# One core, hybrid decoder layer with a PEER expert stage: the activation sums of the expert stage take four PSUM rooms in turn instead of two

## The chip, the core and the metric

The kernel runs on one core of a Trainium2 chip. The metric is the device time of one execution in microseconds (us). Five engines take part: PE (TensorE, the matmul engine), DVE (VectorE), ACT (ScalarE), POOL (GpSimd) and SP (SyncE, which here only issues loads). Matmul sums land in PSUM, which has eight rooms of 128 x 512 float32 values; the kernel names them b0 to b7 in its last part. DVE and ACT read the sums out of PSUM and thereby free the room.

## The reference

One layer on 256 tokens of width 2048. A first part (adaptive norm, one input projection, sparse attention and retention heads, output projection) makes `x`; it is not touched. The second part is a retrieval over 16,384 single-neuron experts:

```
def peer_ffn(h, w_q, sub_keys, w_u, w_v):
    q = (hf @ w_q).reshape(T, PEER_HEADS, 2, PEER_QUERY_DIM // 2)
    s_half = jnp.einsum('thpd,hpkd->thpk', q, sub_keys)
    v_half, i_half = lax.top_k(s_half, K)                # 16 best of 128 keys, twice
    ...
    top_s, pick = lax.top_k(cand_s, K)                   # 16 best of the 256 pairs
    gates = jax.nn.softmax(top_s, axis=-1)
    ...
        a = jnp.einsum('cd,ced->ce', hc, w_u[ec])
        coef = (gc * jax.nn.gelu(a))
        return jnp.einsum('ce,ced->cd', coef, w_v[ec])
```

Each token uses 8 x 16 = 128 experts. The result is gated, added to `x` and normalised.

## The kernel before

Most tokens are not gathered for but computed against all experts: the activations `u @ h` of every expert are formed, passed through gelu, multiplied by a gate matrix that is zero except at the chosen experts, and multiplied with `v`. Of the 256 tokens 160 (`TU`) go this way through `u` and 192 (`TD`) through `v`; the rest are served by gathered rows (`gather`, `steps_`, lines 799 to 869), which POOL fetches by index and DVE multiplies, one 128 x 2048 row block per step (line 844 for `u` rows, 850 for `v` rows).

The expert stage runs in this order: the query projection and the top-k search (lines 1080 to 1151, sums `psA` and `pss`), then for each half `hf` of the 128 expert blocks an activation stage (`u_half`, line 1238) and a value stage (`v_group`, line 897). In short U0, V0, U1, V1.

An activation stage goes through 64 blocks. `u_block` (line 1056) loads 1 MB of `u`, lets PE sum 16 matmuls of 128 x 160 into one room of PSUM (`psU`, line 1062), and has ACT apply gelu, either straight into the result `X` (line 1064, for the columns not yet gated) or into a small buffer `ge` with three places (line 1067), which DVE multiplies into `X` (line 1068). The room is free when ACT has read it.

Between the blocks come the gate groups, eight tokens each: DVE builds one-hot matrices (`o`, lines 1017 to 1020; for the last four groups of a stage `o1m`, `o2m`, `o2n`, lines 1034 to 1037), PE multiplies them into the gate matrix `pg` (line 1047), DVE multiplies it into those columns of `X` that have an activation (line 1052), and ACT copies it into the others (line 1054). In U0 the groups come after the remaining top-k work (`pick`, `gates`, `gates_exp` with an Exp on ACT, line 1179), which DVE does while the first blocks run.

A value stage goes through 64 blocks too: ACT and DVE split 1 MB of `v` into two float32r parts (`whi` line 946, `wlo` line 947), and PE adds 20 matmuls of 128 x 512 into eight sums at once (`acc`, line 964), one in each room: the second token tile's four quarters in b7 to b4, the first tile's in b3 to b0. At the end of V0 the eight sums are copied to SBUF in the order b7, b6 ... b0, ACT and DVE in turn (line 982).

The rooms of PSUM in this part are given out by `bank(kind)` (line 884), with a counter per kind: G (`pg`) takes b2 and b3 in turn, S (small things) b4 and b5, A (`psA`, and before the change `psU`) b6 and b7. Nothing but the value stages' sums uses b0 and b1.

What runs in which order on an engine is fixed before the run by the framework's scheduler, which works from its own estimate of when each room, buffer and operand is free. Some instructions are pinned to the program's order (loads of the stream, gathers, the gathered-row products). Each engine then works through its list strictly in that order.

Of the kernel before, what the change touches and what calls it, by code (L numbers as in the profile page):

```python
# [9 lines left out]
F32 = mybir.dt.float32  # L10
# [10 lines left out]
P = 128  # L21
# [27 lines left out]
TU = TD - NM  # L49
# [66 lines left out]
def body(ctx, tc, a, out, dbg=None, stop=None):  # L116
# [29 lines left out]
    def load(src):  # L146
        r = raw_tile()
        i = nc.sync.dma_start(r, src)
        if ring:
            tc.keep_in_program_order(i)  # L150
        return r
# [88 lines left out]
    def t_block(pool, src_chunk, tag="A", **kw):  # L240
        return t_blocks(pool, [src_chunk], (tag,), **kw)[0]
# [36 lines left out]
    with ExitStack() as fctx:  # L278
# [163 lines left out]
        def n_tile(i, src="winN", tag="A", pace="tile"):  # L442
            ps = [pp.tile([P, 512], F32, name="psN", tag=tag) for _ in range(2)]
            for c in range(4):
                hi, lo = split(load(a[src][i, c].rearrange("p k e -> p (k e)")))
                for kk in range(4):
                    k = 4 * c + kk
                    w = slice(kk * 512, (kk + 1) * 512)
                    for tt in range(2):
                        ts_ = slice(tt * P, (tt + 1) * P)  # L450
                        for j, (x, y) in enumerate(((hh, hi), (hh, lo), (hl, hi))):
                            nc.tensor.matmul(ps[tt], x[:, k, ts_], y[:, w], start=k == 0 and j == 0,  # L452
                                             stop=k == KB - 1 and j == 2)
                background(pace)
            return ps
# [62 lines left out]
        for gp in range(2):  # L518
# [3 lines left out]
            for r in range(4):  # L522
# [37 lines left out]
                f = lambda x: x.rearrange("p a b c d -> p (a b c) d")  # L560
# [142 lines left out]
        for q in range(4):  # L703
            sl = slice(q * 512, (q + 1) * 512)
            ps = n_tile(q, "woutN", "AS"[q % 2], "out")
# [23 lines left out]
        for k in range(KB):  # L729
            with tc.high_priority(offset=(KB - k) * 10):  # L730
                ps = pp.tile([P, 2, P], F32, name="psX", tag="TO"[k % 2])
# [3 lines left out]
                ps = ps.rearrange("p t s -> p (t s)")  # L735
# [8 lines left out]
    with ExitStack() as gctx:  # L744
# [21 lines left out]
        def xb(j):  # L766
            i = sum(j >= b for b in SEG) - 1
            return X[i][:, j - SEG[i], :]
# [115 lines left out]
        def bank(kind):  # L884
            turn[kind] += 1
            return f"b{dict(G=2, S=4, A=6)[kind] + turn[kind] % 2}"
# [169 lines left out]
        def u_block(pool, hf, j, done):  # L1056

            w = load(a["u"][hf * HALF + j].rearrange("p k e -> p (k e)"))
            ps = pool.tile([P, TU], F32, name="psU", tag=bank("A"))
            done = min(done, TU)  # L1060
            for k in range(KB):
                nc.tensor.matmul(ps, w[:, k * P:(k + 1) * P], xT[:, k, 0:TU], start=k == 0, stop=k == KB - 1)  # L1062
            if done < TU:
                nc.scalar.activation(xb(j)[:, done:TU], ps[:, done:TU], AF.Gelu_apprx_tanh)  # L1064
            if done > 0:
                ge = gp_.tile([P, TU], F32, name="ge", bufs=3)
                nc.scalar.activation(ge[:, 0:done], ps[:, 0:done], AF.Gelu_apprx_tanh)  # L1067
                nc.vector.tensor_mul(xb(j)[:, 0:done], xb(j)[:, 0:done], ge[:, 0:done])  # L1068
# [66 lines left out]
        for i in range(16):  # L1135
            ps = first[i] if i < 2 else t_block(up, wq(i), bank("A"), dst=early if i == 2 else None)
# [101 lines left out]
        def u_half(pool, hf, s2, work, budget):  # L1238
            groups[0] = 0
            credit = 0.0  # L1240
            for j in range(HALF):
                u_block(pool, hf, j, groups[0])
                credit += budget if hf or len(work) <= 16 + TD // 8 + 1 else 12.0
                while work and (credit >= work[0][0] or j == HALF - 1):
                    if not hf and j < 28 and len(work) <= TD // 8 + 1:
                        break
                    if not hf and len(work) <= NM // 8 + 1 and plan.index(("u", 1)) > len(plan) - left[0] - 1:
                        break
                    c, f = work.pop(0)
                    credit -= c  # L1250
                    f(j + 1)
                if j == 0:
                    if hf:
                        other[0], most[0] = third_room, 3
                        fetch()
                        set_ring(late, raw=5, whi=3)
                    else:
                        spare[0], other[0], most[0] = s2, more_room, 3
                        set_ring(late, raw=5, whi=3, wlo=2)
                if j == HALF - 10:  # L1260
                    other[0], most[0] = more_room, 3 - hf
                if j == HALF - 4:
                    set_ring(late, raw=5)
                if hf:
                    sparse(j in STEPS["u1"])
                else:
                    if j < 4:
                        rows_m(j)
                    sparse(j in STEPS["u0"])
# [4 lines left out]
        ps = up.tile([P, 512], F32, name="psh", tag=bank("S"))  # L1274
# [41 lines left out]
```

## Time and profile before

| | us |
|---|---|
| median of 3 runs (lowest, highest) | 1898.67 (1896.92, 1903.09) |
| the profiled execution, its own time | 1908.31 |
| the profiled execution, its span | 1906.5 |
| U0, first activation matmul to first value matmul | 688.1 to 996.5 |
| V0 | 996.5 to 1289.0 |
| U1 | 1289.0 to 1581.2 |
| V1, up to the last value matmul | 1581.2 to 1876 |
| PE busy, of the span | 1818.3 (95%) |

The profiled execution is one run; 1.8 us of its time lie around its span. All places below are in microseconds from the start of the span. A row of the timeline gives start, length, engine, line, operation, destination and sources, the number of instructions merged, and in brackets how long the engine idled before it and on what. One activation matmul of the code appears as two records in the trace, so a block of 16 is 32 records.

### The profile page before, as it was taken

Reading aid. Unit: us, or ns where it says so; the run is one execution under the profiler, and the core shown is the slowest. Engines: PE = TensorE matmul, PEld = TensorE weight load, DVE = VectorE, ACT = ScalarE, POOL = GpSimd, SP = SyncE. Lnnn points to the kernel's source line nnn. Section 1 sums busy time; section 2 is a strip of 40 time slices with the busy share of each in tenths; the row PEclk is TensorE's granted clock in tenths of the full one; section 3 lists DMA queues with packets and bytes.
Section 4 is the critical chain, followed back from the end, with each engine's and each line's share of the span. In section 5 each row is a group of like instructions: output and inputs, shape, how many; then the busy total and the mean of one; then the engine's idle time right before and its main releaser. Section 6 shows DMA issues by size and latency. Waiting matters only on the chain.

```text
span 1906.5 us, 28615 instructions
## 1 busy us (share of the span) xinstructions
PE 1818.3 (95%) x11303; PEld 1590.0 (83%) x11303; DVE 1480.8 (78%) x2333; ACT 708.4 (37%) x1279; POOL 370.8 (19%) x256
## 2 busy tenths in 40 slices
PE   5899999999998999999999999999999999999995
PEld 4899878788777898999997777779999997777773
DVE  7988877889788998677478899983455558988875
ACT  3444443635435421021025555541111114555542
POOL 1000001011000012102123343331111114544210
PEclk9999899999998999999999999999999999999998
DMA  8999877889797879988989999989999989999981
GB/s 350 373 328 370 303 278 225 314 286 350 288 352 259 318 292 355 410 352 338 382 318 380 416 411 418 415 322 425 375 357 365 347 328 382 418 384 391 382 300 45
DMA packets 94474, 652.93 MB, mean 342 GB/s; under 512 B 11410, under 2 KB 11618, under 8 KB 18434
## 3 DMA queue, kind: packets, MB, share of 16 engines
q1 hardware_dynamic: 66818, 467.78, 64.1%
q0 software_dynamic: 27520, 183.32, 24.5%
q8 instruction: 89, 1.46, 0.3%
q14 instruction: 47, 0.38, 0.1%
HBM read 644.97 MB, written 4.22 MB: 341 GB/s over the span
## 4 chain that ended last, share of the span: by engine, by line
PE 78%; DVE 13%; DMA 5%; issue 2%; ACT 1%; POOL 0%; SPq 0%; ACTq 0%; POOLq 0%; DVEq 0%
PE acc L964 31%; PE psU L1062 25%; PE psN L452 8%; DMA raw<-in_adaT 3%; DVE wlo L158 2%; PE bkB L353 2%; DVE raw L198 2%; PE psD L353 2%; PE bkC L353 1%; PE bvB L405 1%; PE psA L236 1%; PE pg L1047 1%; DMA raw<-in_winA 1%; PE pT L548 1%; PE sc L538 1%
## 5 line engine op out<-in xcount | busy, mean ns | idle before, releaser
L1062 PE MATMUL psU<-xT,raw 128*128 128x160 f32 x4096 | 573.1, 301 | 6.7 <-ACT X L1064 4.2
L1062 PEld LDWEIGHTS psU<-xT,raw 128*128 128x128 f32 x4096 | 561.6, 191 | 7.9 <-ACT X L1064 4.7
L964 PE MATMUL acc<-whi,cc 128*128 128x512 f32 x1512 | 367.9, 391 | 0.0
L947 DVE TENSOR_TENSOR wlo<-raw,whi 128x2048 fp32r<-128x2048 f32 x126 | 288.0, 2286 | 71.2 <-issue 57.8
L964 PEld LDWEIGHTS acc<-whi,cc 128*128 128x128 f32 x1512 | 283.8, 188 | 68.9
L964 PE MATMUL acc<-wlo,cc 128*128 128x512 f32 x1008 | 252.8, 391 | 2.4 <-DVE wlo L947 2.4
L946 ACT CAST whi<-raw 128x2048 fp32r<-128x2048 f32 x126 | 240.7, 1911 | 0.0
L157 ACT CAST whi<-raw 128x1024 fp32r<-128x1024 f32 (+1 forms) x174 | 168.5, 1017 | 187.2 <-PE psN L452 42.9
L198 DVE SCALAR_TENSOR_TENSOR raw<-raw,crow 128x2048 f32<-128x2048 f32 x96 | 219.1, 2284 | 23.6 <-DMA raw<-in_adaT 23.5
L158 DVE TENSOR_TENSOR wlo<-raw,whi 128x1024 fp32r<-128x1024 f32 (+1 forms) x174 | 200.8, 1180 | 27.4 <-ACT whi L157 27.3
L964 PEld LDWEIGHTS acc<-wlo,cc 128*128 128x128 f32 x1008 | 161.8, 161 | 63.6 <-DVE wlo L947 3.2
L452 PE MATMUL psN<-whi,act 128*128 128x512 f32 x512 | 172.3, 413 | 1.3 <-ACT whi L157 1.1
L1068 DVE TENSOR_TENSOR X<-X,ge 128x160 f32<-128x160 f32 (+19 forms) x94 | 25.8, 275 | 163.3 <-ACT ge L1067 161.3
L1064 ACT ACTIVATE X<-psU 128x160 f32<-128x160 f32 (+19 forms) x102 | 25.5, 252 | 320.7 <-PE psU L1062 308.7
L452 PEld LDWEIGHTS psN<-whi,act 128*128 128x128 f32 x512 | 97.9, 194 | 27.1 <-issue 3.2
L452 PE MATMUL psN<-wlo,act 128*128 128x512 f32 x256 | 104.6, 411 | 3.9 <-DVE wlo L158 3.9
L941 ACT CAST cc<-X 128x192 fp32r<-128x192 f32 x128 | 44.7, 353 | 138.9 <-PE acc L964 137.8
L803 POOL DMA_INDIRECT rows<-in_urow,sx x32 | 69.3, 2165 | 135.5 <-DVE rows L844 122.1
L236 PE MATMUL psA<-act,whi 128*128 128x512 f32 x240 | 87.0, 403 | 2.9 <-ACT whi L157 2.9
L803 POOL DMA_INDIRECT xT<-in_v,sx x21 | 62.8, 2992 | 107.4 <-DVE cc L942 63.2
L948 ACT CAST cc<-cc 128x64 fp32r<-128x64 f32 x128 | 31.2, 244 | 134.8 <-DVE cc L942 134.5
L353 PE MATMUL psD<-act,whi 128*128 128x256 f32 x384 | 73.6, 292 | 1.3 <-ACT whi L157 1.3
(350 smaller groups left out, 2564.6 us busy)
## 6 DMA issues: line engine op xcount, KB each, us to landing
raw<-in_u SPq DMA_DIRECT2D x128, 1024.0 KB
raw<-in_v SPq DMA_DIRECT2D x128, 1024.0 KB
raw<-in_adaT SPq DMA_DIRECT2D x96, 1024.0 KB
raw<-in_winN SPq DMA_DIRECT2D x16, 1024.0 KB
raw<-in_woutN SPq DMA_DIRECT2D x16, 1024.0 KB
raw<-in_wqT SPq DMA_DIRECT2D x16, 1024.0 KB
raw<-in_winB SPq DMA_DIRECT2D x16, 832.0 KB
raw<-in_winD SPq DMA_DIRECT2D x12, 1024.0 KB
```

The lines of the kernel that those rows point to most:

```text
L157: nc.scalar.copy(hi[:, sl], r[:, sl])
L158: nc.vector.tensor_sub(lo[:, sl], r[:, sl], hi[:, sl].bitcast(F32))
L198: nc.vector.scalar_tensor_tensor(r, r, 1.0, crow, op0=OP.mult, op1=OP.mult, accum_out=modc[:, j, k:k + 1])
L236: nc.tensor.matmul(p_, hi[:, sl], act[:, k], start=k == 0, stop=False, skip_group_check=True)
L353: nc.tensor.matmul(bank[:, b, :], x[:, w], y[:, k, :], start=k == k0 and n == 0 and first, stop=k == k1 - 1 and n == 2, skip_group_check=True)
L452: nc.tensor.matmul(ps[tt], x[:, k, ts_], y[:, w], start=k == 0 and j == 0, stop=k == KB - 1 and j == 2)
L803: pin(nc.gpsimd.indirect_dma_start(out=r, out_offset=None, in_=src, in_offset=bass.IndirectOffsetOnAxis(ap=o, axis=0)))
L941: inorder(nc.scalar.copy(ch, xb(j)))
L946: inorder(nc.scalar.copy(hi, r))
L947: nc.vector.tensor_sub(lo, r, hi.bitcast(F32))
L964: nc.tensor.matmul(acc[c][0:m], x, w[:, c[1] * 512:(c[1] + 1) * 512], start=jj == 0 and n == 0, stop=jj == HALF - 1 and n == 2 - c[0], ski ...
L1062: nc.tensor.matmul(ps, w[:, k * P:(k + 1) * P], xT[:, k, 0:TU], start=k == 0, stop=k == KB - 1)
```

## The change

One line: the room of an activation sum is chosen by the block's number, and no longer by the counter of kind A.

```
         def u_block(pool, hf, j, done):
             w = load(a["u"][hf * HALF + j].rearrange("p k e -> p (k e)"))
-            ps = pool.tile([P, TU], F32, name="psU", tag=bank("A"))
+            ps = pool.tile([P, TU], F32, name="psU", tag=f"b{(0, 1, 6, 7)[j % 4]}")
```

A sum may now stay unread while three more blocks are summed, where it was one. Each stage starts with b0 and b1 (blocks 0 and 1), which V0 uses until its very end. The query projection keeps b6 and b7.

The lists of SP and POOL are the same, instruction by instruction. Those of PE, DVE and ACT move in U0 and at the seams between the stages. Before U0, three and then four matmuls of block 0 stand ahead of the last two query projections, and one pair of score matmuls (`pss`) stands behind the last one instead of in its middle.

The first place is PE's list in U0, among the gate groups (`o_7354` to `o_7407` are the one-hot operands of the groups number 10 to 12 of 24):

```order
 L1047 LDWEIGHTS o_7352
 L1047 MATMUL pg<-o_7354,o_7352 128x64
-L1062 MATMUL psU<-xT,raw 128x160 x3
+L1062 MATMUL psU<-xT,raw 128x160 x22
 L1047 LDWEIGHTS o_7405
 L1047 MATMUL pg<-o_7407,o_7405 128x64
-L1062 MATMUL psU<-xT,raw 128x160 x7
```

More activation matmuls stand ahead of the same group. Counted over the whole list, the first group stands behind 464 activation matmuls of U0 in both kernels; the nineteenth stands behind 617 before and behind 646 now; the four last groups, which need the gathered rows of the first kind, begin behind 893 before and behind 930 now, and end behind 946 and 973 of the 1024.

The second place is PE's list where U1 follows V0 (`acc` are the value sums of V0, `o_10778` to `o_10833` the one-hots of the first two groups of U1):

```order
 L964 MATMUL acc_8667<-wlo,cc 128x512
 L964 MATMUL acc_8668<-wlo,cc 128x512
-L1062 MATMUL psU<-xT,raw 128x160 x80
 L1047 LDWEIGHTS o_10778
 L1047 MATMUL pg<-o_10780,o_10778 128x64
@@ -4743,5 +4744,5 @@
 L1047 LDWEIGHTS o_10778
 L1047 MATMUL pg<-o_10780,o_10778 128x64
-L1062 MATMUL psU<-xT,raw 128x160 x48
+L1062 MATMUL psU<-xT,raw 128x160 x16
 L1047 LDWEIGHTS o_10831
 L1047 MATMUL pg<-o_10833,o_10831 128x64
```

PE now begins U1 with the first gate group (16 matmuls into b3); then come the 16 matmuls of block 1 (into b1), six of the second group (b2), block 0 (b0) and on.

The third place is DVE's list at the same seam, where it copies its four sums of V0 (`acc_8662` in b6, `acc_8664` in b4, `acc_8666` in b2, `acc_8668` in b0):

```order
 L982 COPY s_6165<-acc_8662 128x512
+L844 SCALAR_TENSOR_TENSOR rows,dots<-rows,h2t 128x2048
 L982 COPY s_6165<-acc_8664 128x512
 L982 COPY s_6165<-acc_8666 128x512
 L982 COPY s_6165<-acc_8668 128x512
-L844 SCALAR_TENSOR_TENSOR rows,dots<-rows,h2t 128x2048
-L844 SCALAR_TENSOR_TENSOR raw,dots<-raw,h2t 128x2048 x2
```

A gathered-row product now stands between the first of the copies and the three others. In V0 itself DVE's list has two of these products fewer ahead of the copies (84 in all from the start, where it was 86).

## The prediction

> **What bounds the kernel now.** I read the page first, then PE's waits, then the timeline around each wait. The page's busy line, the part of the chain that ended last, and the group of the activation matmuls:
>
> ```profile
> PE 1818.3 (95%) x11303; PEld 1590.0 (83%) x11303; DVE 1480.8 (78%) x2333; ACT 708.4 (37%) x1279; POOL 370.8 (19%) x256
> PE acc L964 31%; PE psU L1062 25%; PE psN L452 8%; DMA raw<-in_adaT 3%; DVE wlo L158 2%; PE bkB L353 2%; DVE raw L198 2%; PE psD L353 2%; PE bkC L353 1%; PE bvB L405 1%; PE psA L236 1%; PE pg L1047 1%; DMA raw<-in_winA 1%; PE pT L548 1%; PE sc L538 1%
> L1062 PE MATMUL psU<-xT,raw 128*128 128x160 f32 x4096 | 573.1, 301 | 6.7 <-ACT X L1064 4.2
> ```
>
> PE sets the end, and the last number is the most that more rooms can take out of idle time before these matmuls: 6.7 us in 573. The waits of PE name their parts (total, times, longest):
>
> ```profile
> PE psU L1062 <- ACT X L1064: 4.2, 2, 4.0
> PE psU L1062 <- ACT ge L1067: 2.5, 1, 2.5
> PE acc L964 <- DVE wlo L947: 2.4, 1, 2.4
> PE pg L1047 <- DVE o L1020: 0.4, 1, 0.4
> ```
>
> So there are two stalls for a room, 4.0 and 2.5 us, both in U0; U1 has none. The first, in the timeline:
>
> ```profile
> 740.09 0.30 ACT L1064 ACTIVATE X<-psU 128x160 f32<-128x160 f32 x1 [4.04 <-PE psU L1062]
> 741.79 6.96 PE L1062 MATMUL psU<-xT,raw 128*128 128x160 f32 x50
> 750.77 0.31 ACT L1179 ACTIVATE gt<-gt 128x128 f32<-128x128 f32 x1 [9.07 <-DVE gt L1172]
> 752.39 0.50 ACT L1064 ACTIVATE X<-psU 128x160 f32<-128x160 f32 x2
> 752.75 7.51 PE L1062 MATMUL psU<-xT,raw 128*128 128x160 f32 x41 [4.00 <-ACT X L1064]
> ```
>
> ACT stood at the Exp of the gates until DVE's top-k work delivered `gt` at 750.8. Behind it in ACT's list waited two blocks' activations. PE filled both rooms by 748.75 and stood.
>
> The second, at 855 (ACT's evacuation, then PE again):
>
> ```profile
> 855.15 0.26 ACT L1067 ACTIVATE ge<-psU 128x104 f32<-128x104 f32 x1
> 855.46 1.63 PE L1062 MATMUL psU<-xT,raw 128*128 128x160 f32 x6 [2.51 <-ACT ge L1067]
> ```
>
> Here ACT's evacuation stood behind copies of gate groups that a busy DVE had to release.
>
> **The change part by part.** (1) The first stall. A block lasts 4.35 us, the distance of two evacuations in steady state:
>
> ```profile
> 767.77 0.30 ACT L1064 ACTIVATE X<-psU 128x160 f32<-128x160 f32 x1 [4.04 <-PE psU L1062]
> 772.12 0.30 ACT L1064 ACTIVATE X<-psU 128x160 f32<-128x160 f32 x1 [4.04 <-PE psU L1062]
> ```
>
> Two more rooms let PE go on for 2 x 4.35 = 8.7 us while ACT stands, and it stood 4.0 us too long: all of it goes, with the 0.2 us at the earlier Exp. Gain 4.2. If DVE delivered `gt` up to 4.7 us later than now, the cover would still hold. What could make it later is the pair of `pss` that moves behind the last query projection:
>
> ```profile
> 682.24 0.61 PE L1089 MATMUL pss<-raw,pq 128*128 128x128 f32 x4
> 688.09 0.98 PE L1062 MATMUL psU<-xT,raw 128*128 128x160 f32 x6
> ```
>
> It comes 5.9 us later, and 1.9 more for the seven matmuls of part 4 (7 x 4.35/16). If DVE had nothing else to do, `gt` would be 7.8 us late and PE would stand 3.1; it has the other score tables and `pick` meanwhile, so I take 0.
>
> (2) The second stall. In this stretch the chain runs over DVE, not PE (start, length):
>
> ```profile
> 838.12 0.67 DVE o L1020 x2
> 840.29 2.21 DVE s L844 x2
> ...
> 881.72 0.60 PE pg L1047 x15
> 882.32 7.69 PE psU L1062 x56
> ```
>
> So free rooms alone don't help; PE must also have activation matmuls ahead of the groups that DVE hasn't made. The new order has them. The first group runs at 824.5 (DVE waited for it, so the stretch moves with PE), the nineteenth is through at 882.3: 57.9 us that DVE's work needs. In the new order 646 - 464 = 182 activation matmuls and 18 groups stand between: 182 x 4.35/16 = 49.5, and 18 x 0.63 (the row below) = 11.3, together 60.8 us of PE work. That is longer than DVE needs, so PE no longer waits there: gain 2.5, and the 0.4 before a group stays in my sum as an uncertain extra. If DVE's pace still holds PE, the gain here is 0.
>
> ```profile
> 841.01 0.63 PE L1047 MATMUL pg<-o,o 128*128 128x64 f16 x16
> 824.46 0.93 PE pg L1047 x32
> ```
>
> (3) The clock. After each stall PE runs at half clock for a while (busy time and records of each engine, then the granted clock):
>
> ```profile
> 748.00:753.00 5.00, 1.00 (x8) 0.76 (x7) 4.69 (x13) 2.09 (x4) 1.03 (x1) 1.00 0.99 419
> 753.00:757.00 4.00, 4.00 (x19) 4.00 (x19) 4.00 (x7) 0.00 (x0) 0.94 (x1) 0.57 1.01 428
> 757.00:761.00 4.00, 4.00 (x32) 4.00 (x31) 4.00 (x8) 0.30 (x1) 0.00 (x0) 1.00 1.01 426
> 851.00:855.00 4.00, 1.38 (x31) 1.07 (x30) 3.93 (x12) 1.40 (x5) 0.00 (x0) 1.00 1.00 412
> 855.00:859.00 4.00, 3.54 (x15) 3.43 (x16) 3.96 (x9) 0.60 (x3) 0.73 (x1) 0.61 0.10 43
> ```
>
> In 4 us PE issued 19 records in place of 32 and the clock was 0.57; the time lost is (1 - 0.57) x 4 = 1.7 us. After the second stall, (1 - 0.61) x 4 = 1.6. Without the stalls the clock has no reason to drop: gain 3.3, bounds 0 and 3.3. [...]
>
> (4) The moves before U0. Seven matmuls of block 0 go ahead of the last two query projections. PE has no hole there to fill, so they gain nothing; they could only cost a wait for block 0's load. That load was issued at 660.6, and the DMA engines had fallen still by 665, before the first of the moved matmuls' place (669):
>
> ```profile
> 660.58 0.33 SPq L148 DMA_DIRECT2D raw<-in_u  x1
> 665.00:667.00 2.00, 2.00 (x14) 1.75 (x13) 2.00 (x8) 0.80 (x2) 0.00 (x0) 1.00 0.00 0
> ```
>
> Cost 0.
>
> (5) The seam V0 to U1, where the new rooms are the last to come free:
>
> ```profile
> 1287.82 1.76 ACT L982 COPY s<-acc 128x512 f32<-128x512 f32 x3 [0.34 <-PE acc L964]
> 1288.28 1.89 DVE L982 COPY s<-acc 128x512 f32<-128x512 f32 x3 [0.24 <-PE acc L964]
> 1288.99 6.27 PE L1062 MATMUL psU<-xT,raw 128*128 128x160 f32 x45
> 1291.10 2.29 DVE L844 SCALAR_TENSOR_TENSOR rows<-rows,h2t 128x2048 f32<-128x2048 f32 x1 [0.94 <-DMA rows<-in_urow,sx]
> raw<-in_urow,sx POOLq DMA_INDIRECT x4, 12.7
> ```
>
> On this trace's times: ACT frees b3 one copy of 0.6 before its last one ends, at 1289.0, and b1 at 1289.6; the first group (0.63) takes PE to 1289.7, block 1 to 1294.1, six matmuls of the second group to 1294.3. DVE's first copy ended at 1288.04, 0.24 before the others began. With the row product of 2.3 us behind it and copies of 0.7, DVE frees b2 at about 1291.7 and b0 at 1292.4, ahead of need. So 0 to 0.3, if the gathered rows have landed. If not, DVE stands and its copies with it, beyond a cover of 1.9 us; a gather here takes 12.7 us to land, so the upper bound is 11 us (the rival below). Nothing says that these rows are late, so I stay near the lower end, with 0.6.
>
> (6) V1's start moves by one row product of 2.3 us earlier or later on DVE against the split that PE waits 2.4 us for: 0, bounds -2.4 and +2.4. Blocks 60 and 61 leave b0 and b1 two blocks, 8.7 us, before a value stage wants them: 0. SP's and POOL's lists are unchanged; block 1 being used before block 0 delays the reuse of one load's buffer by 4.35 us, with five loaded ahead: 0.
>
> The sum: -4.2 - 2.5 - 3.3 + 0.6 = -9.4 us, from a span of 1906.5 to 1897.1. V0, U1 and V1 start earlier by it, and PE bounds them. The profiled execution took 1908.3, 9.6 over the median of the runs; I take the same difference off the median: 1898.7 - 9.4 = 1889.3.
>
> **The rivals.** *Half of it*: DVE's pace still holds PE at 882, so part 2 and its half clock give nothing: -4.2 - 1.7 + 0.6 = -5.3, 1893.4. For it speaks the chain above, against it the 60.8 against 57.9. *Given back in V0*: what U0 gains is lost because V0 cannot begin or run earlier:
>
> ```profile
> 1100.00:1120.00 20.00, 20.00 (x89) 15.37 (x88) 18.94 (x17) 9.30 (x12) 8.88 (x4) 1.00 1.01 419
> SPq L148 <- DVE cc L942: 92.5, 21, 9.0
> ```
>
> DMA is at its full share and DVE at 18.9 of 20. Against it: over 100 us the loads waited 92.5 us for a buffer that V0's own work frees, so they follow PE. Or the last gate groups, which need gathered rows that come no earlier, hold PE. Time 1898. *Slower*: the seam. If the rows in front of DVE's copies are gathered only about when PE ends V0, they land 12.7 us later at 1301; with 2.3 and three copies of 0.7, b0 is free at 1305 where PE wants it at 1294.3. It decides from about 5 us after V0's end; at full size PE stands 11 us and loses some 2 to half clock, net +3.6 with the gain off, 1902. Against it: 84 products are done by then, and at most three gathers are kept in flight. *Clock by rooms*: going round more rooms makes PE pause at the change from one to the next, and the clock drops. With two rooms in turn there is no pause:
>
> ```profile
> 800.00:820.00 20.00, 20.00 (x150) 20.00 (x149) 6.90 (x6) 1.21 (x4) 2.81 (x3) 1.00 1.01 425
> ```
>
> If four rooms lost 1.7 us to half clock at every eighth of the 128 blocks, that would be 27 us: 1916. [...]
>
> **How the numbers follow.** Forecast 0.59, half of it 0.18, given back 0.14, seam 0.07, clock 0.02. A measurement tells about 0.3% (5.7 us) from no change, so the forecast and 0.07 of the second case count as faster: 0.66. The rest of it, the third and 0.03 of the seam, of which only the worst passes 0.3%, are the same: 0.28. Slower is 0.06. The range holds the forecast with V1's bound downward (1889.3 - 2.4, and the 0.4, and about 1 of measurement: 1885.5) and the second case and part of the third upward, to 1897.
>
> **What would show it.** Right: PE's waits for `psU` on ACT gone from 4.2 and 2.5 to under 1 together; clock 1.00 from 750 to 860; U0 shorter by about 10 us; U1's first block within 1 us of the first group. Wrong: PE waiting for `pg` on DVE between 820 and 960, a wait for `psU` on DVE's copies at U1's start, or V0 longer by what U0 gained.

## The result and the profile after

| | before | changed |
|---|---|---|
| median of 6 runs each, side by side, us | 1901.83 (1896.92 to 1909.65) | 1889.66 (1887.06 to 1895.85) |
| ratio | | 0.9945, 95% interval 0.9927 to 0.9963 |
| profiled execution, its time and span, us | 1908.31, 1906.5 | 1895.85, 1894.1 |
| last query projection (L236) to V0's first sum (L964), us | 308.8 | 295.7 |
| V0, first to last sum, us | 292.2 | 292.2 |
| V0's last sum to V1's first, us | 292.4 | 292.7 |
| V1, first to last sum, us | 295.1 | 293.3 |
| from there to the end, us | 30.2 | 30.2 |

The changed kernel is faster by 0.55%: 10.5 us, with 7.0 to 13.9 in the interval. The forecast was 1889.3. The lower rows of the table say where: the stage U0, 13.1 us shorter by this measure, and V1, 1.8 shorter. Of the 13.1, 1.9 are not a gain: seven matmuls of block 0 (0.272 us each) now stand ahead of the last query projection, so that this much of U0 is done when the count begins. That leaves 11.2 in U0.

The changed kernel's page, the same three lines as before: busy time, the chain's lines, the group of the activation matmuls.

```profile
PE 1816.1 (96%) x11303; PEld 1589.3 (84%) x11303; DVE 1479.9 (78%) x2333; ACT 708.7 (37%) x1279; POOL 379.5 (20%) x256
...
PE acc L964 31%; PE psU L1062 28%; PE psN L452 8%; PE psD L353 3%; DMA raw<-in_adaT 2%; PE bkB L353 2%; PE psA L236 2%; DVE raw L198 2%; DVE wlo L158 2%; PE pg L1047 1%; PE bkC L353 1%; PE bvB L405 1%; PE psA L237 1%; DMA raw<-in_winA 1%; PE pT L548 1%
...
L1062 PE MATMUL psU<-xT,raw 128*128 128x160 f32 x4096 | 569.9, 300 | 0.0
```

The idle time ahead of the activation matmuls went from 6.7 us to 0.0, and their busy time from 573.1 to 569.9: that is half clock that is gone. PE holds 28% of the chain in this line where it held 25%. Of PE's waits in the stages that the change touches, two are left:

```profile
PE ptr L1190 <- DVE ex L1128: 0.8, 1, 0.8
...
PE acc L964 <- DVE wlo L947: 0.6, 1, 0.6
```

Both waits of `psU` on ACT and the 0.4 of `pg` on DVE are gone, and the wait at V1's start is 0.6 where it was 2.4. The wait of `ptr` on DVE, in U0, was 0.3 us before and is 0.8 now. The windows around the two old stalls, in the changed kernel (busy time and records of PE, PEld, DVE, ACT and POOL, then granted clock, DMA share, GB/s):

```profile
748.00:753.00 5.00, 5.00 (x39) 5.00 (x38) 4.65 (x13) 1.55 (x2) 1.03 (x1) 1.00 1.00 423
753.00:757.00 4.00, 4.00 (x32) 4.00 (x31) 4.00 (x6) 0.84 (x4) 0.94 (x1) 1.00 1.02 430
850.00:855.00 5.00, 5.00 (x50) 4.96 (x49) 4.97 (x14) 1.36 (x5) 1.15 (x1) 1.00 0.60 193
855.00:860.00 5.00, 5.00 (x68) 4.88 (x63) 5.00 (x11) 1.64 (x6) 0.00 (x0) 1.00 1.01 385
```

PE is busy throughout at clock 1.00; in 753 to 757 it issues 32 records where it issued 19. What it does not show is a faster ACT. ACT's own timeline in the changed kernel:

```profile
751.43 0.31 ACT L1179 ACTIVATE gt<-gt 128x128 f32<-128x128 f32 x1 [8.96 <-DVE ti L1075]
751.76 1.28 ACT L1064 ACT_TABLE_LOAD   x1
753.05 0.50 ACT L1064 ACTIVATE X<-psU 128x160 f32<-128x160 f32 x2
753.90 0.30 ACT L1064 ACTIVATE X<-psU 128x160 f32<-128x160 f32 x1 [0.35 <-PE psU L1062]
```

ACT still stands 9 us at the gates' Exp. Then it evacuates two blocks at once, and a third 0.35 us later, as soon as PE has finished it: PE was summing into a third room while two sums stood unread, which two rooms do not allow.

### The profile page after: what moved, and what is told of

It reads as the page before. It is cut to its first block, busy times and chain, and to the rows that moved or that the text cites. A ratio compares the mean times of both kernels' runs of the same rounds, so it can differ in the third digit from the quotient of the medians.

```text
span 1894.1 us, 28604 instructions
## 1 busy us (share of the span) xinstructions
PE 1816.1 (96%) x11303; PEld 1589.3 (84%) x11303; DVE 1479.9 (78%) x2333; ACT 708.7 (37%) x1279; POOL 379.5 (20%) x256
## 4 chain that ended last, share of the span: by engine, by line
PE 84%; DVE 9%; DMA 3%; issue 2%; ACT 1%; POOL 0%; SPq 0%; ACTq 0%; POOLq 0%; DVEq 0%
PE acc L964 31%; PE psU L1062 28%; PE psN L452 8%; PE psD L353 3%; DMA raw<-in_adaT 2%; PE bkB L353 2%; PE psA L236 2%; DVE raw L198 2%; DVE wlo L158 2%; PE pg L1047 1%; PE bkC L353 1%; PE bvB L405 1%; PE psA L237 1%; DMA raw<-in_winA 1%; PE pT L548 1%
## 5 line engine op out<-in xcount | busy, mean ns | idle before, releaser
L1062 PE MATMUL psU<-xT,raw 128*128 128x160 f32 x4096 | 569.9, 300 | 0.0
L964 PE MATMUL acc<-whi,cc 128*128 128x512 f32 x1512 | 367.8, 391 | 0.0
L964 PEld LDWEIGHTS acc<-whi,cc 128*128 128x128 f32 x1512 | 283.8, 188 | 68.9
L964 PE MATMUL acc<-wlo,cc 128*128 128x512 f32 x1008 | 252.5, 391 | 0.6 <-DVE wlo L947 0.6
L964 PEld LDWEIGHTS acc<-wlo,cc 128*128 128x128 f32 x1008 | 162.0, 161 | 61.6 <-DVE wlo L947 1.3
L1064 ACT ACTIVATE X<-psU 128x160 f32<-128x160 f32 (+19 forms) x102 | 25.6, 253 | 306.3 <-PE psU L1062 298.3
L236 PE MATMUL psA<-act,whi 128*128 128x512 f32 x240 | 87.9, 407 | 3.2 <-ACT whi L157 3.2
L803 POOL DMA_INDIRECT s<-in_urow,sx x26 | 57.5, 2213 | 134.6 <-DVE s L844 101.9
L844 DVE SCALAR_TENSOR_TENSOR rows<-rows,h2t 128x2048 f32<-128x2048 f32 x32 | 73.1, 2286 | 3.5 <-DMA rows<-in_urow,sx 3.5
```

The source lines that it names most:

```text
L236: nc.tensor.matmul(p_, hi[:, sl], act[:, k], start=k == 0, stop=False, skip_group_check=True)
L803: pin(nc.gpsimd.indirect_dma_start(out=r, out_offset=None, in_=src, in_offset=bass.IndirectOffsetOnAxis(ap=o, axis=0)))
L844: pin(nc.vector.scalar_tensor_tensor(r, r, 1.0, h, op0=OP.mult, op1=OP.mult, accum_out=d[:, e:e + 1]))
L964: nc.tensor.matmul(acc[c][0:m], x, w[:, c[1] * 512:(c[1] + 1) * 512], start=jj == 0 and n == 0, stop=jj == HALF - 1 and n == 2 - c[0], ski ...
```

## The experiments

The theory on trial: two stalls of PE for a room in U0, each with half clock behind it; the first is ACT standing in order at the Exp, the second DVE's pace among the gate groups, for which PE has too little other work ahead. The rivals are named with each run.

Two things to know when reading. A profile's time of day is not comparable between kernels: the last query projection lay anywhere from 676 to 690 us in the twelve profiles, with differing stretches of half clock around 560 to 590 (the granted clock over 570 to 600 is 0.72 in before, 0.77 in the changed kernel, 0.89 in U1-only), ahead of everything that the change touches. So U0 is read as a length, from the last query projection's last `whi` matmul to V0's first sum, and the V0 start times in the first four expectations are read as such lengths. And kernels with the seven early matmuls of block 0 show 1.9 us too little (0.3 with one); the third column of the table adds it.

| kernel | ratio to before, 95% interval | U0 us, with early matmuls | waits of psU, pg us | lost at half clock in U0, us | V1 us (its first wait) |
|---|---|---|---|---|---|
| before | | 308.8 | 6.7, 0.4 | 3.4 | 295.1 (2.4) |
| changed | 0.9945 [0.9927, 0.9963] | 297.6 | 0, 0 | 0 | 293.3 (0.6) |
| four rooms in U0 only | 0.9926 [0.9899, 0.9952] | 297.6 | 0, 0 | 0 | 293.3 (0.6) |
| four rooms in U1 only | 1.0006 [0.9984, 1.0028] | 307.0 | 4.9, 0.4 | 3.3 | 295.1 (2.4) |
| four rooms, early blocks | 0.9981 [0.9961, 1.0001] | 304.7 | 2.5, 0.4 | 3.1 | 296.5 (2.4) |
| four rooms, late blocks | 0.9943 [0.9923, 0.9964] | 300.0 | 2.7, 0 | 0 | 293.3 (0.6) |
| three rooms | 0.9978 [0.9963, 0.9993] | 301.3 | 1.0, 1.8 | 0 | 296.1 (1.9) |
| before, no Exp on ACT | 0.9988 [0.9973, 1.0003] | 305.5 | 4.5, 0 | 3.0 | 293.4 (0.6) |
| changed + DVE load | 0.9951 [0.9932, 0.9970] | 299.2 | 1.0, 0.3 | 0 | 293.3 (0.6) |
| before + DVE load | 1.0034 [1.0013, 1.0054] | 312.9 | 2.0, 7.6 | 4.9 | 296.3 (2.2) |
| two other rooms | 1.0001 [0.9973, 1.0029] | 306.3 | 5.5, 0.4 | 1.6 | 294.6 (1.9) |
| rooms in the order 6, 7, 0, 1 | 0.9937 [0.9916, 0.9959] | 297.2 | 0, 0 | 0 | 293.3 (0.6) |

"Lost at half clock" is half of the time for which PE was busy in U0 while its granted clock was 0.50. With this loss and all idle time of PE taken off, the third column is 296.4 to 298.1 us in all twelve profiles: waits and half clock are what these kernels differ by in U0. In three profiles V1 is longer than its first wait accounts for. With the early blocks the granted clock is 0.73 over 1578 to 1582, right behind that wait, and 0.85 over the next 4 us, which makes V1 1.7 us longer. With three rooms V1 is 296.1 us where two other rooms, with the same first wait of 1.9, have 294.6, and before + DVE load has 296.3 with a shorter wait than before's.

**Which stage.** Four rooms in U0 alone, then in U1 alone (the same edit with `hf == 1`):

```
-    tag=f"b{(0, 1, 6, 7)[j % 4]}"
+    tag=f"b{(0, 1, 6, 7)[j % 4]}" if hf == 0 else bank("A")
```

> Four rooms in U0 only; U1 goes round two rooms as before. Theory (the gain is two stalls of PE in U0 with the half clock behind each): V0's first sum starts at 985 to 987 us, as with the whole change (985.7; before 996.5), no wait of psU on ACT in U0, and the time is 10 to 11 us under before; the stretch from U1's first matmul to the last of V1 stays at before's 587 us. Rival (U1 and V1 take part: the 1.6 us that they became shorter come from the four rooms of U1): the same in U0, and nothing else; then U1 with V1 must go back from 585.7 to 587.3.

> Four rooms in U1 only; U0 as before. Theory: U0 keeps both stalls (4.2 and 2.5 us of waits of psU on ACT) and V0 starts at 996 to 997 us; the time is within 0.2% of before, at most 2.4 us under it. Rival (the rooms of U1 give the 1.6 us of U1 and V1 by themselves): U1 with V1 585.7 instead of 587.3, time 1.6 us under before.

U0 alone gives all of it: U0 297.6 as in the changed kernel, median 1886.82 against 1899.03. U1 alone gives nothing, 1.0006. Both rivals asked where the 1.8 us of V1 come from, and the answer is not U1: V1 is 293.3 us with four rooms in U0 only and 295.1 with four in U1 only. Here the expectation for U0 alone missed, its rival with it: from U1's first matmul to V1's last should have taken before's 587 us and took 585.5, as in the changed kernel (585.6). The 1.8 us come with a change in U0, a stage and a half earlier, through the order of PE's list (below). In U1-only, U0 is that of before, and its first stall came out smaller than in the profile that I had sized it from:

```profile
PE psU L1062 <- ACT ge L1067: 2.5, 1, 2.5
PE psU L1062 <- ACT X L1064: 2.4, 2, 2.2
```

The first stall is 2.2 us here and 4.0 in the profile of before. The second is 2.5 in both.

**Which blocks.** The early ones (the stretch of the Exp), then the late ones (that of the gate groups):

```
+    tag=f"b{(0, 1, 6, 7)[j % 4]}" if hf == 0 and j < 22 else bank("A")     # early
+    tag=f"b{(0, 1, 6, 7)[j % 4]}" if hf == 0 and j >= 22 else bank("A")    # late
```

> Four rooms in U0 for blocks 0 to 21 only, ahead of the gate groups; the other blocks of U0 and all of U1 use two. Theory (two separate stalls, each with its own half clock): the first stall goes with its half clock, the second stays at about 2.5 us; V0 starts 4.2 + 1.7 = 5.9 us earlier, at 990.6, and the time is 5.9 us under before. Rival A (DVE's pace sets when the groups can run, whenever PE comes to them): what PE gains ahead of the groups it waits for later; the stall at 855 grows by 5.9 to some 8 us and V0 starts at 996. Rival B (the clock costs nothing of its own): 4.2 us, V0 at 992.3.

> Four rooms in U0 for blocks 22 to 63 only, through the stretch of the gate groups; blocks 0 to 21 and all of U1 use two. Theory: the first stall stays at 4.0 us with its half clock, the second goes with its own: 2.5 + 0.4 + 1.6 = 4.5 us, V0 starts at 992, time 4.5 us under before. Rival A (DVE's pace holds PE there): nothing is gained, V0 at 996, with a wait of pg on DVE in the place of the second stall. Rival B (the clock costs nothing of its own): 2.9 us, V0 at 993.6.

Early blocks alone: the first stall is gone, the second is exactly the old one.

```profile
PE psU L1062 <- ACT ge L1067: 2.5, 1, 2.5
PE acc L964 <- DVE wlo L947: 2.4, 1, 2.4
...
PE pg L1047 <- DVE o L1020: 0.4, 1, 0.4
```

So rival A, by which the second stall would grow to 8 us, falls. The time gained 0.2% (3.6 us, interval -0.2 to 7.4), less than the 5.9 expected, which the interval holds. U0 is 304.7, that is 4.1 under before's profile, 2.3 under the one with four rooms in U1 alone. Three things eat into it. The stall that it removes is smaller in the other profiles than in the one of before. V1 has the half clock named under the table, 1.7 us. And the half clock behind the second stall was twice as long in this execution, 6.8 us up to 849.4, with PE back at 843.2; its middle:

```profile
844.00:846.00 2.00, 2.00 (x10) 1.88 (x9) 2.00 (x4) 0.11 (x1) 0.03 (x1) 0.50 0.00 0
846.00:848.00 2.00, 2.00 (x9) 2.00 (x9) 1.38 (x4) 0.16 (x1) 1.01 (x1) 0.50 0.29 53
```

Late blocks alone: PE's waits in U0 are those of the first stall only.

```profile
PE psU L1062 <- ACT X L1064: 2.7, 2, 2.5
PE acc L964 <- DVE wlo L947: 0.6, 1, 0.6
```

The second stall and the wait of `pg` are gone, and no wait of `pg` on DVE took their place, so rival A falls here as well. But the gain, 10.8 us with an interval of 6.8 to 14.6, is more than the 4.5 expected. The profile shows two reasons. V1 is 1.8 shorter, which I had not counted. And what stays of the first stall is cheap: 2.5 us, and no half clock behind it. Beside four rooms in U1 only, whose U0 is that of before, U0 is 7.0 us shorter and V1 1.8; these 8.8 the interval holds. PE stands until 750.56 in this kernel, and then:

```profile
746.00:750.00 4.00, 2.03 (x15) 1.79 (x14) 3.82 (x12) 1.40 (x2) 1.03 (x1) 1.00 1.01 426
750.00:754.00 4.00, 3.44 (x25) 3.44 (x26) 3.87 (x6) 0.69 (x3) 0.94 (x1) 1.00 1.01 426
754.00:758.00 4.00, 4.00 (x32) 4.00 (x31) 4.00 (x6) 0.30 (x1) 0.00 (x0) 1.00 1.01 426
```

The clock is 1.00 throughout. Rival B (the clock costs nothing of its own) is thus right for the first stall of this execution; it is wrong for the second, behind which the clock fell in all six profiles with two rooms in the late blocks (0.61 over 4 us in before, the others below). By its time this kernel can't be told from the changed one (0.9943 and 0.9945); its U0 is 2.4 us longer, which is the first stall.

**Is it the Exp?** The kernel before, with two rooms and nothing on ACT that waits for the gates:

```
-    nc.scalar.activation(gt, gt, AF.Exp)
+    nc.vector.tensor_scalar(gt, gt, -0.5, 1.0, op0=OP.max, op1=OP.add)
```

> The kernel before, two rooms, with the gates' Exp left out: a clamp and an addition on DVE stand in its place (so the gates aren't the reference's), and ACT waits for nothing there. Theory (the first stall is ACT standing in order at this Exp while both rooms are full): the first stall and its half clock go, the second stays at about 2.5 us (619 matmuls ahead of the nineteenth group, 617 before); from the last query projection to V0 302 to 304 us, as with four rooms in the early blocks alone (302.8). Rival (PE stands there for another reason, such as DVE or the loads): 307 to 309 us and a wait of 2 to 4 us near 750.

```profile
741.65 0.30 ACT L1064 ACTIVATE X<-psU 128x160 f32<-128x160 f32 x1 [4.04 <-PE psU L1062]
746.00 0.30 ACT L1064 ACTIVATE X<-psU 128x160 f32<-128x160 f32 x1 [4.04 <-PE psU L1062]
750.35 0.30 ACT L1064 ACTIVATE X<-psU 128x160 f32<-128x160 f32 x1 [4.04 <-PE psU L1062]
```

ACT evacuates a block every 4.35 us through the whole stretch, and PE has no wait there, with two rooms. So the first stall is ACT standing in order at this Exp, whose two table loads of 1.28 us (last section) are gone with it in this run. The length missed its range, 305.5 where 302 to 304 were expected. One reason is the yardstick: the 302.8 that I set it beside has seven matmuls ahead and is 304.7 on the same footing. The other is that the second stall did grow here:

```profile
PE psU L1062 <- ACT ge L1067: 4.5, 1, 4.5
```

It is 4.5 instead of 2.5 us, and 6.8 us of half clock, 3.0 us lost, lie behind it. That is a part of rival A's idea: among the groups DVE's pace counts, and a PE that comes earlier may wait longer there.

**Does DVE's pace count, and PE's work as its cover?** Three rooms change how far PE's list can run ahead of the groups; a doubled one-hot makes DVE slower in them.

```
+    tag=f"b{(0, 6, 7)[j % 3]}"                                             # three rooms
...
     nc.vector.tensor_tensor(two(o1), io(0, P), bc(idx[:, 0], P), op=OP.is_equal)
+    if hf == 0:                                                            # DVE load
+        nc.vector.tensor_tensor(two(o1), io(0, P), bc(idx[:, 0], P), op=OP.is_equal)
```

> Three rooms (b0, b6, b7) in U0 and U1. PE's list has 631 activation matmuls ahead of the nineteenth gate group where before has 617 and the change 646. Theory (a wait of PE among the groups is what DVE needs from the first to the nineteenth, 57.9 us, less PE's own work there): one room more covers 4.35 us of ACT's standstill, so the first stall (2.2 to 4.0 us in the profiles of before's U0 up to now) goes; among the groups PE's work is 167 x 0.272 + 18 x 0.63 = 56.7 us, so some 1.2 us of waiting stays, and up to 1.7 us of half clock with it. From the last query projection to V0 297 to 299 us (before 308.8 and 307.0, the change 295.7). Rival (only free rooms count, the order of the groups doesn't): no wait at all, 295.7.

> The changed kernel with one DVE instruction more in each gate group of U0: the first one-hot is written twice, 0.61 us a group, 11 us over the 18 groups. PE's list now has 670 activation matmuls ahead of the nineteenth group. Theory (PE's work among the groups is the cover for DVE's): DVE needs 57.9 + 11.0 = 68.9 us, PE has 206 x 0.272 + 11.3 = 67.3 us, so PE waits about 1.6 us there (and may lose up to 1.7 at half clock); from the last query projection to V0 297 to 299 us (295.7 without the load). Rival A (DVE's pace sets the stretch whatever PE has ahead of the groups): 11 us longer, 306.7. Rival B (free rooms alone cover it): 295.7.

> The kernel before with the same DVE instruction more in each gate group of U0. PE's list has 643 activation matmuls ahead of the nineteenth group. Theory: DVE needs 68.9 us, PE has 179 x 0.272 + 11.3 = 60.0 us, so waits and half clock among the groups come to 8.9 us, where they are 4.5 to 5 without the load; from the last query projection to V0 311 to 313 us (307.0 and 308.8 without the load). Rival (DVE doesn't limit the stretch; the stall of 2.5 us is one late copy): 307 to 309.

Three rooms, PE's waits:

```profile
PE pg L1047 <- DVE o L1020: 1.8, 2, 0.9
PE psU L1062 <- ACT ge L1067: 1.0, 1, 1.0
```

The first stall is gone with one room more, and among the groups 2.8 us of waiting are left where 1.2 were expected and the rival said none. U0 is 299.4 by the count of the expectation, 0.4 over its range, and 3.7 above the changed kernel. The load on DVE, with four rooms:

```profile
PE psU L1064 <- ACT ge L1069: 1.0, 1, 1.0
...
PE pg L1049 <- DVE o L1022: 0.3, 1, 0.3
```

and with two:

```profile
PE pg L1049 <- DVE o L1022: 7.6, 3, 4.0
...
PE psU L1064 <- ACT X L1066: 2.0, 1, 2.0
```

With four rooms 11 us more of DVE work cost 1.6 us (297.3 after 295.7, by the expectation's count), with 1.3 us of waits against 1.6 worked out. With two rooms the waits among the groups went from 2.9 to 7.6 us and the loss at half clock there from 1.6 to 3.2, U0 is 312.9 where 311 to 313 were expected, and the time rose by 0.34%. From the first gate group's start to the nineteenth's it takes 57.0 us with two rooms, 59.0 with three and 59.0 with four; with the load 70.3 with two and 67.6 with four. More rooms don't shorten this stretch, and PE waits in it whenever it has too little other work: DVE's pace is a floor under it, and the rooms decide how much of it PE fills with activation matmuls. Both rivals on the changed kernel (all 11 us shown, or none) fall.

**Number of rooms, or which rooms?** Two others, and the same four in another order:

```
+    tag=f"b{j % 2}"                        # two other rooms
+    tag=f"b{(6, 7, 0, 1)[j % 4]}"          # another order
```

> Two rooms again, but b0 and b1 in place of b6 and b7, in U0 and U1. PE's list has the same 617 activation matmuls ahead of the nineteenth gate group as before. Theory (the number of rooms counts, and with it the order that it allows): both stalls stay, 2 to 4 us near 750 and 2.5 us near 850, each with half clock behind it or not; from the last query projection to V0 305 to 309 us, the time within 0.3% of before. Rival (which rooms counts: b6 and b7 are shared with the query projections and the tail, b0 and b1 are not): 296 to 300 us, faster by 0.4% or more.

> Four rooms in the order b6, b7, b0, b1, so that each stage starts with the two rooms that it always had. Theory: U0 as with the change (the same number of matmuls ahead of each group), 295 to 297 us from the last query projection to V0; at the seam from V0 to U1, where the change was found to wait for nothing, nothing is won, under 0.3 us; the time is within 0.2% of the change, 0.3 to 0.8% under before. At V1's start PE's list has 8 whi matmuls behind block 0's last wlo matmul, as in the change, so the wait there should be near its 0.6 us. Rival (b0 and b1, the last rooms that V0 gives back, cost the change something at the seam): U1's first matmul comes earlier by up to 1 us after V0's end.

Two other rooms are as good as the old two, 1.0001. Both stalls are there, 2.8 and 2.5 us. U0, 304.4 by the expectation's count, is 0.6 under its range; with the 1.9 us of early matmuls it is 306.3, inside. The number counts. The other order is no different from the change in anything that can be measured: 0.9937 with an interval that holds 0.9945. V0's last sum to V1's first takes 292.5 us, against 292.7 in the change and 292.4 before: the seam cost the change 0.2 to 0.3 us. No kernel is faster than the changed one by more than the intervals: with no wait for a room left in U0, more rooms or other rooms have no such wait to remove (more than four were not run).

## Why the prediction was right

**Part 1, the first stall**: right in its cause (the kernel without the Exp on ACT) and in its cure (three rooms do). Its size was that of one execution. In the five profiles with two rooms in the early blocks and the Exp in place (before, U1-only, late blocks, two other rooms, before + DVE load) the waits of `psU` on `X` are 4.2, 2.4, 2.7, 3.0 and 2.0 us, 2.9 on the mean. It goes with DVE. From the last query projection to the Exp are 63.1, 61.3, 61.6, 60.3 (62.2 with its early matmuls) and 61.0 us, and PE's stall, 4.0, 2.2, 2.5, 2.8 and 2.0, is in all five what that exceeds 59.1 by, within 0.3. In the changed kernel it is 61.4, or 63.3 with the early matmuls, so by the same count two rooms would have cost it 4.2. `gt` comes 0.2 later by it than in before's profile, with the `pss` pair moved: well inside the 4.7 of cover.

**Part 2, the second stall**: right. Gone together with the 0.4 of `pg`, in the changed kernel and with late blocks alone. The margin was thinner than the prediction had it. Its 57.9 us of DVE ran to the end of the nineteenth group and its 60.8 us of PE only to its start; to the start it is 57.1 in before's profile, and the changed kernel has 59.0. With three rooms the stretch took 59.0 too, 2.8 of it waits, so PE's work in the changed kernel just covers it. The three tests with less cover or more load came out within 2 us of the same arithmetic. In every run without the DVE load free rooms and the new order came together, so what either would do alone is not shown.

**Part 3, the clock**: right for the second stall. All six profiles with two rooms in the late blocks have half clock behind it (granted clock 0.61 over 4 us in before, 0.66 in U1-only, 0.65 with two other rooms; 0.50 over 844 to 848 with the early blocks, over 840 to 844 without the Exp and over 848 to 852 with the load), and the six without the stall have none there (1.00 over 850 to 860 in the changed kernel). For the first stall it was too much: two of the five profiles have no half clock behind it (late blocks and two other rooms, granted clock 1.00), which makes 1.0 us on the mean instead of 1.7.

**Parts 4 and 5**: nothing before U0, as said; in U0 the wait of `ptr` on DVE grew by 0.5 us, which the sum doesn't have. At the seam 0.2 to 0.3 us instead of 0.6: the gathered rows that stand ahead of DVE's copies had landed, `b0` came free in time, and PE waited for nothing.

**Part 6, V1's start**: taken as 0 with bounds of 2.4 either way, measured 1.8 us of gain. The mechanism was not the one named (a row product earlier or later on DVE). It is where the last `wlo` matmul of V1's first block stands in PE's list. Before:

```profile
1585.44 2.23 PE L964 MATMUL acc<-whi,cc 128*128 128x512 f32 x9
1587.50 0.40 PE L964 MATMUL acc<-wlo,cc 128*64 128x512 f32 x1
1587.93 2.29 DVE L947 TENSOR_TENSOR wlo<-raw,whi 128x2048 fp32r<-128x2048 f32 x1 [5.79 <-PE acc L964]
1590.28 1.88 PE L964 MATMUL acc<-wlo,cc 128*128 128x512 f32 x7 [2.38 <-DVE wlo L947]
```

Changed:

```profile
1573.41 1.99 PE L964 MATMUL acc<-wlo,cc 128*128 128x512 f32 x8
1575.24 2.00 PE L964 MATMUL acc<-whi,cc 128*128 128x512 f32 x8
1575.49 2.29 DVE L947 TENSOR_TENSOR wlo<-raw,whi 128x2048 fp32r<-128x2048 f32 x1 [1.71 <-issue]
1577.84 2.10 PE L964 MATMUL acc<-wlo,cc 128*128 128x512 f32 x8 [0.61 <-DVE wlo L947]
```

Before, one of the eight `wlo` matmuls stands behind nine `whi` ones of the next block, at 1587.5; only after it may DVE write the next `wlo` into that buffer, 5.8 us after it was ready to. In the changed kernel all eight stand together, eight `whi` matmuls follow, and DVE writes while PE does those. The wait goes by how many `whi` matmuls stand behind the last of the eight `wlo` ones: none in before, U1-only and early blocks (2.38 us), one in before + DVE load (2.16), two with three rooms and with two other rooms (1.93), eight in the other six (0.61). Each covers 0.22 us. One of those six is the kernel without the Exp, which has two rooms throughout: it is the order of the list that counts here, and not the rooms themselves. Why the scheduler moves this matmul after a change in U0 stays open.

So the sum with measured sizes is 2.9 + 1.0 for the first stall, 2.9 + 1.6 for the second, 1.8 at V1's start, less 0.3 at the seam and 0.5 at `ptr`: 9.4 us, against 10.5 (7.0 to 13.9) by the times. That this is the forecast's own 9.4 is in part luck: the first stall and its clock were 2.0 us too much and the 0.5 was not seen, while V1's start gave 1.8 more, the wait of `pg` 0.4 more and the seam cost 0.3 less than was summed. That 1889.3 lies 0.4 us from the median is in part luck as well: it started from 1898.67, the median of three runs of the kernel before, whose six runs beside the changed kernel have 1901.83. Of the rivals, "half of it" and "given back" fall with the late blocks and with V0's unchanged 292.2 us, "slower at the seam" with 0.3 us there (its net +3.6 had the seam's 0.6 in it twice; +3.0 gives 1902 as well), "clock by rooms" with the group's mean of 300 ns, before 301, and no idle time ahead of these matmuls; its loss at every eighth block was an assumption, which no run shows.

## What to carry to other kernels

A stall that one profile shows has that execution's size: before counting on it, find what its length depends on (here how late DVE delivers, less a constant) and look at a second execution. Half clock stood behind such a stall in some executions and not in others (behind the first stall in three of five profiles; next section), so count it as a chance. More buffers between two engines paid twice here, once by covering a consumer that stands in order behind a slow producer (the stall of 2.0 to 4.0 us at the Exp), and once by letting the order put more work ahead of a slow third engine (the 2.5 us among the groups); an extra load on that engine shows which of the two holds. And changing the rooms of one stage can reorder another far behind it, so compare the stage lengths over the whole span.

## What the runs showed of the hardware

**The clock after a short stall.** The same kind of stall, PE idle for 2.0 to 4.0 us, is followed by half clock in some profiles and not in others. In before's it is both times: PE is back at 752.75 and at 855.46, and the windows behind are

```profile
753.44:756.86 3.42, 3.42 (x15) 3.42 (x15) 3.42 (x6) 0.00 (x0) 0.94 (x1) 0.50 1.01 429
756.86:760.27 3.41, 3.41 (x27) 3.41 (x27) 3.41 (x6) 0.30 (x1) 0.00 (x0) 1.00 1.01 425
...
855.85:859.26 3.41, 3.41 (x16) 3.29 (x15) 3.38 (x6) 0.26 (x1) 0.99 (x1) 0.50 0.04 17
859.26:862.67 3.41, 3.41 (x50) 3.33 (x50) 2.42 (x8) 0.62 (x2) 0.05 (x1) 1.00 0.79 250
```

With two other rooms both cases are in one profile. Its two long stalls, and the windows in which they end and those behind:

```profile
747.49 12.76 PE L1062 MATMUL psU<-xT,raw 128*128 128x160 f32 x92 [2.78 <-ACT X L1064]
...
PE psU L1062 <- ACT ge L1067: 2.5, 1, 2.5
...
744.00:748.00 4.00, 1.22 (x9) 0.98 (x8) 3.69 (x13) 2.09 (x4) 1.03 (x1) 1.00 1.01 428
748.00:752.00 4.00, 4.00 (x32) 4.00 (x31) 4.00 (x8) 0.00 (x0) 0.94 (x1) 1.00 1.01 426
...
845.00:849.00 4.00, 1.24 (x18) 1.05 (x19) 4.00 (x13) 1.52 (x5) 0.00 (x0) 0.92 0.83 334
849.00:853.00 4.00, 4.00 (x21) 3.88 (x21) 3.77 (x7) 0.26 (x1) 1.04 (x1) 0.65 0.01 4
```

The first stall is the longer one, 2.78 us, and the clock stayed at 1.00; behind the second, 2.5 us, it was 0.65 over 4 us. V1's first wait of 2.38 us shows both cases too: in before the clock is 1.00 from 1585 to 1598, with the early blocks it is 0.73 over 1578 to 1582. So the length of the stall alone doesn't tell the cases apart in these profiles. Nor was PE idle before every fall: ahead of U0, with other shapes of matmul, the changed kernel has

```profile
277.05:280.46 3.41, 3.41 (x28) 2.79 (x28) 2.37 (x3) 0.48 (x1) 0.00 (x0) 1.00 0.79 255
280.46:283.87 3.41, 3.41 (x12) 2.93 (x13) 3.29 (x16) 1.37 (x6) 0.00 (x0) 0.50 0.87 315
```

What decides it was not shown.

**The table load in the stall.** The changed kernel's rows of ACT have an ACT_TABLE_LOAD of 1.28 us between the Exp and the next evacuation, and before's trace has the same at 751.10. The load for the Exp itself runs while ACT waits for `gt` anyway (in before at 740.41, the Exp at 750.77), but the way back stands in PE's stall of 2 to 4 us. No run changed this alone.
